# Every matmul operand in SBUF at one offset: split weights in tiles of 4096 bytes, SBUF pools in another order, a pad ahead of them

## The chip, the cores and the metric

The kernel runs on one core of a Trainium2 chip. The metric is the device time of one execution in microseconds (us), the median of several runs. The profile is one further execution, taken by the hardware profiler.

## The reference

A batch of one, 512 tokens by 1024 features, goes through two layers of a hybrid block and then one block of a second kind. All arrays are float32.

```python
# first block, twice (l = 0, 1)
mod = silu(c) @ w_ada[l] + b_ada[l]; shift, scale, gate = split(mod, 3)
h = rms_norm(x, norm_g[l]) * (1 + scale) + shift
gq, gk, gv, glr, gz, dq, dk, dv, dz = split_columns(h @ w_in[l])
gq, gk, gv = split(silu(causal_depthwise_conv([gq, gk, gv], conv_w[l])))
o_gla  = gla_branch(gq, gk, gv, glr, gz, ...)     # gated linear attention, chunks of 64
o_diff = diff_branch(dq, dk, dv, dz, ...)         # softmax maps p0 - lam * p1, 4 heads
x = x + gate * ([o_gla, o_diff] @ w_out[l])
# second block, once
x = x + 0.5 * swiglu(rmsnorm(x, ffn1_norm), ffn1_w_in, ffn1_w_out)      # D_FF = 2816
x = x + hybrid_mixer(rmsnorm(x, mix_norm), w_in, ..., w_out)
x = x + 0.5 * swiglu(rmsnorm(x, ffn2_norm), ffn2_w_in, ffn2_w_out)
return rmsnorm(x, final_norm)
```

Nearly all of the arithmetic lies in the products with weights: w_in and w_out of the two layers, the two feed-forwards, and the seven projections of the mixer.

## The kernel before

**Products in three passes.** A float32 product is made of three float32r matmuls (`mm3`, lines 163 to 167). Every operand is split in a high and a low part; the three are high by high (L165), one low by high (L166 or L167), and the other. The activations are split by `split` into slots, tiles of 512 float32 (2048 bytes) of the pool `sp`. The weights come in 1 MB transfers, one for each job, into tiles of the pool `wraw`, and `weights` (lines 131 to 145) splits them in pieces: ScalarE writes the high part (L141), VectorE the low part (L142), into two tiles of the pool `wsp`, tags `hi` and `lo`, four buffers each.

**Two forms of product.** In `fm1` (feature-major, tiles named `fm`) the stationary operand is a slice of 128 columns, 512 bytes, of a weight piece, and the moving operand a slot of activations of 512 columns. In `tm` (token-major, tiles named `tm`) it is the other way: a quarter of a slot is stationary, and 512 (or 264) columns of a weight piece move. A piece of a usual job is 8 slices of 128 columns in `fm1`, so 24 matmuls of 512 columns; in `tm` it is 2 slices by 4 token tiles by 3, also 24.

**Order.** `run` interleaves one stream of large products with light tasks (attention, linear attention, norms, modulation), by costs and due times in the code; the order of the instructions on each engine is then set by the tile scheduler. While job i runs, the pieces of job i + 1 are loaded and split. A new `hi` or `lo` tile waits until the matmuls on its buffer's earlier contents are done.

**Where the operands lie.** SBUF is given out in the order of the pools: `const`, `xp`, `wraw`, `wsp`, `sp`, `small`. An address here is the byte in each partition, as it stands in the built program. The slots of `sp` begin at 120736 and follow each other by 2048 bytes, so that each is 416 modulo 512. A `hi` or `lo` tile has 1056 columns, 4224 bytes, which is 8 x 512 + 128, so its four buffers begin at four different places modulo 512:

| buffer | before | modulo 512 | after the change | modulo 512 |
|---|---|---|---|---|
| hi | 86944, 91168, 95392, 99616 | 416, 32, 160, 288 | 45472, 49568, 53664, 57760 | 416, 416, 416, 416 |
| lo | 103840, 108064, 112288, 116512 | 416, 32, 160, 288 | 61856, 65952, 70048, 74144 | 416, 416, 416, 416 |
| slots | 120736 + 2048 n | 416 | 78240 + 2048 n | 416 |

The slices of a piece follow each other by 512 bytes (2048 in `tm`), so a whole piece keeps its place modulo 512. From the first feed-forward on the buffers are taken in turn: `hi` at 86944 (416), 99616 (288), 95392 (160), 91168 (32), and again. The `lo` part lies at 416 and 288 where `hi` does, at 32 where `hi` is at 160, and at 160 where `hi` is at 32.

**The odd width.** The 1056 columns are those of a piece of `wvg` (value projection and low-rank gate input, two jobs in each layer): a job has two pieces of 4 x 264 columns, `[(4, 264)] * 2`.

Of the kernel before, what the change touches and what calls it, by code (L numbers as in the profile page):

```python
# [16 lines left out]
P = 128  # L17
# [10 lines left out]
# columns of the packed vectors, each 128 values down the partitions  # L28
# [38 lines left out]
LG = 4.5  # L67


@with_exitstack  # L70
def block_kernel(ctx: ExitStack, tc: tile.TileContext, a, out):
# [3 lines left out]
    wraw = ctx.enter_context(tc.tile_pool(name="wraw", bufs=RAW))  # L75
    wsp = ctx.enter_context(tc.tile_pool(name="wsp", bufs=4))
    sp = ctx.enter_context(tc.tile_pool(name="sp", bufs=SLOTS))
    small = ctx.enter_context(tc.tile_pool(name="small", bufs=8))
    pp = ctx.enter_context(tc.tile_pool(name="pp", bufs=8, space=bass.MemoryType.PSUM))
    # the tensor engine takes its products in the order in which they are written here  # L80
# [45 lines left out]
    # 1 + the bias of the scale  # L126
# [4 lines left out]
    def weights(src, shapes, eng=V):  # L131
        """pieces [128, kts, n] of one transfer, each in its two parts; and the pieces themselves"""
        total = sum(k * n for k, n in shapes)
        raw = wraw.tile([P, 2112], F32, tag="raw", name=nm("raw"))
        nc.sync.dma_start(raw[:, 0:total], src)
        at, pieces = 0, []
        for k, n in shapes:
            src_p = raw[:, at:at + k * n]
            hi = wsp.tile([P, 1056], F32R, tag="hi", name=nm("hi"))[:, 0:k * n]
            lo = wsp.tile([P, 1056], F32R, tag="lo", name=nm("lo"))[:, 0:k * n]  # L140
            A.activation(hi, src_p, AF.Copy)  # L141
            eng.tensor_tensor(lo, src_p, f(hi), op=ALU.subtract)  # L142
            pieces.append(tuple(v.rearrange("p (k n) -> p k n", n=n) for v in (hi, lo, src_p)))
            at += k * n
        return pieces
# [4 lines left out]
    def split(src, s="sp", width=S, scale=None):  # L150
        """float32 tile -> its two parts; `scale`: a column that multiplies it"""
        hi = slot(s + "h", F32R)
        lo = slot(s + "l", F32R)
        h, l = hi[:, 0:width], lo[:, 0:width]
        if scale is None:
            A.activation(h, src, AF.Copy)
            V.tensor_tensor(l, src, f(h), op=ALU.subtract)
        else:
            A.activation(h, src, AF.Copy, scale=scale)
            V.scalar_tensor_tensor(l, src, scale, f(h), op0=ALU.mult, op1=ALU.subtract)  # L160
        return hi, lo

    def mm3(o, wh, wl, ah, al, start, stop):
        """o += (wh + wl).T @ (ah + al), without wl.T @ al: 2 ** -24 of a product, its rounding in float32"""
        T.matmul(o, wh, ah, start=start, stop=False)  # L165
        T.matmul(o, wh, al, start=False, stop=False)  # L166
        T.matmul(o, wl, ah, start=False, stop=stop)  # L167

    # ---- the order of the tensor engine's work: one stream of large products, and light tasks
    # between them. Both are generators; they yield the time that their products take, the light  # L170
    # ones also the time (or the event) before they go on ----
# [39 lines left out]
    st = {}  # L211

    def rsqrt(o, src, n, scale):
        """o = (src * scale + EPS) ** -0.5, src in SBUF or PSUM"""
        m = tiny([P, 8], "rin", bufs=8)
        V.tensor_scalar(m[:, 0:n], src, scale, EPS, op0=ALU.mult, op1=ALU.add)  # L216
        G.tensor_tensor(o, m[:, 0:n], mhalf[:, 0:n], op=ALU.pow)  # L217
# [9 lines left out]
    def norm(d0, d1):  # L227
        """a light task: column form [tok, 4] and row form [128, tok] of the inverse root"""
        yield 0, d0
        acc = st["acc"]  # L230
        ps = psum("nps")
        for t in range(NT):
            T.matmul(ps[:, t:t + 1], acc[:, t * P:(t + 1) * P], ones[:, 0:1], start=True, stop=True)
        rs = tiny([P, NT], "rs", bufs=2)
        rsqrt(rs, ps[:, 0:NT], NT, 1.0 / D)
        st["rs"] = rs
        rh, rl = tiny([P, NT], "rh", F32R, bufs=2), tiny([P, NT], "rl", F32R, bufs=2)
        V.tensor_copy(rh, rs)
        V.tensor_tensor(rl, rs, f(rh), op=ALU.subtract)
        yield 0.9, d1  # L240
        pb = psum("nbc")
        for t in range(NT):
            for i, r in enumerate((rh, rl)):
                T.matmul(pb[:, t * P:(t + 1) * P], r[:, t:t + 1].to_broadcast([P, P]), identr, start=i == 0, stop=i == 1)
        st["pb"] = pb
        bc = slot("rsb")
        A.activation(bc, pb, AF.Copy)
        st["bc"] = bc
        yield 1.7, 0
# [25 lines left out]
    def residual(o, k, scale, nxt):  # L275
        """x += scale o; the sum of squares and what the next stage reads follow"""
        V.scalar_tensor_tensor(xs[k], o, scale, xs[k], op0=ALU.mult, op1=ALU.add)
        after(k, nxt)
# [12 lines left out]
    mods = [(const.tile([P, 24], F32, name=f"mod{l}"), const.tile([P, 8], F32, name=f"gs{l}")) for l in range(L)]  # L291

    def ada_load(l, j, parts=1):
        """the weights of two columns a partition, of features 128 j on and 128 (j + 1) on"""
        w = wraw.tile([P, 2112], F32, tag="raw", name=nm("ada"))[:, 0:2 * D].rearrange("p (i r) -> p i r", r=D)
        for i in range(0, 2, 2 // parts):
            n = 2 // parts
            nc.sync.dma_start(w[:, i:i + n], a["ada"][l, j // 2][:, i:i + n])
        return w
# [6 lines left out]
    def mod_of(l, j, w):  # L306
        """of features 128 (j % 8) on: the shift, 8 on the scale, 16 on the gate"""
        mod, gs = mods[l]
        t, i = dot(w), j - 8
        if 0 <= i < 8:  # L310
            V.scalar_tensor_tensor(
                gs[:, i:i + 1], t, bg1[:, 8 * l + i:8 * l + i + 1], col("norm_g", 8 * l + i), op0=ALU.add, op1=ALU.mult)
        else:
            V.tensor_tensor(mod[:, j:j + 1], t, col("b_ada", 24 * l + j), op=ALU.add)
        st["mod", l, j] = True

    def modulation(which, pause):
        """a light task"""
# [8 lines left out]
    def lambdas():  # L327
        """a light task"""
        lamv = const.tile([64, 8], F32, name="lamv")
        nc.sync.dma_start(lamv, a["lamv"])  # L330
        for l in range(L):
# [7 lines left out]
            # -lam  # L339
# [6 lines left out]
    def head_norm(o, z, zi, gcol, y, yi, scales=None):  # L346
        """`scales`: columns that multiply the head's values"""
# [26 lines left out]
    def layer_jobs(l):  # L374
# [6 lines left out]
        def vectors():  # L381
            # small scaled vectors
# [4 lines left out]
            # taps [tile, tap]; what the silu's halves and the query's scale need goes into them  # L387
# [7 lines left out]
        def feat(k, eng):  # L395
            """x times the inverse root and the scale; and the shift"""
# [5 lines left out]
        # q, k of the softmax branch: normed over each 64  # L402
# [32 lines left out]
        # -- the first product(s) --  # L435
        if l == 0:
            # x times gain goes in as the scales come; the shift's part follows
# [15 lines left out]
            def q_part(k0, k1):  # L453
                def body(_):
# [4 lines left out]
                    for k in range(k0, k1):  # L459
# [7 lines left out]
                        if k % 2 == 0:  # L467
                            w["wh"] = tuple(wsp.tile([P, 1056], F32R, tag=v, name=nm(v)) for v in ("hi", "lo"))
# [107 lines left out]
        else:  # L576
            # x times gain goes in before the norm is known; the norm and the shift's product follow
# [36 lines left out]
        # -- v of the softmax branch and the gates' low-rank input --  # L614
# [30 lines left out]
        jobs += [(a["wvg"][l, b], [(4, 264)] * 2, vjob(b)) for b in range(2)]  # L645

        # -- softmax attention --
# [6 lines left out]
        def attention():  # L654
            qk, r0 = {}, {}

            def scores(hd, i):
                n = (i + 1) * P
                es, rr = [], []
                # the two maps lie in different halves of the array and run side by side  # L660
# [7 lines left out]
                for m in range(2):  # L668
# [10 lines left out]
                    else:  # L679
                        # the second's weight against the first's  # L680
# [45 lines left out]
        # -- gated linear attention --  # L726
        def gla():
# [48 lines left out]
            for c in range(4):  # L776
# [12 lines left out]
                # states of two heads (64 + 64 partitions) after each chunk  # L789
# [34 lines left out]
        # -- the rest of the large products --  # L824
# [8 lines left out]
        def z_job(dst, j0):  # L833
            # 2 silu(z)
# [17 lines left out]
        # -- output: the heads that are ready first go first --  # L852
# [3 lines left out]
        def wo_job(c):  # L856
            def body(ps):
                if c < 2:
                    # four tiles at once, with the heads as they come
# [31 lines left out]
    def ffn_jobs(i, nxt):  # L891
# [31 lines left out]
        # the last two tiles of the last stage, and what follows, take one half of the tokens at a time  # L923
# [34 lines left out]
        def last_norm(hs, sqs):  # L958
            """tokens down the partitions"""
# [34 lines left out]
    def mixer_jobs():  # L994
# [76 lines left out]
        # tanh(z / 2) + 1, twice the sigmoid, times the projection of one branch  # L1071
# [76 lines left out]
def _pack(i):  # L1148
# [4 lines left out]
    def chunk(w):  # L1153
        """[K, n] -> [128, (K / 128) n]: what a partition reads lies together"""
# [3 lines left out]
    def tiles(w):  # L1158
        """the same for each 128 columns in turn"""
        return np.concatenate([chunk(w[:, j:j + P]) for j in range(0, w.shape[1], P)], axis=1)  # L1160

    def cv(v):
        """a vector, 128 values down the partitions"""
# [75 lines left out]
```

## Time and profile before

| | |
|---|---|
| time, median of 3 runs | 1765.99 us (1765.78 to 1766.84) |
| the profiled execution, span of its instructions | 1762.7 us |
| TensorE (PE) busy | 1730.3 us, 98% |
| weight loads (PEld) | 1409.5 us, 80% |
| VectorE (DVE), ScalarE (ACT), GpSimd (POOL) | 54%, 38%, 5% |
| bytes from HBM | 178.00 MB, 102 GB/s over the span |

The profile gives each instruction's start and duration. Matmuls are pipelined: one that is listed with 0.39 us is followed by the next some 0.23 us later. So what a stream of matmuls costs is read from the distance of their starts and not from their durations. A weight load stands under PEld, beside the matmul that runs at the time. The profiled execution's span is 3.3 us below the median of the runs, which is what lies around it.

### The profile page before, as it was taken

The page shows a single profiled execution, that of the slowest core. Times are in us where ns is not written, and L with a number is a line of the kernel's source. Part 1 is how long each engine was busy: PE and PEld are TensorE (multiplying, and loading weights), DVE is VectorE, ACT ScalarE, POOL GpSimd, SP SyncE. Part 2 cuts the span into 40 slices and gives each one's busy share as a digit, 9 for nine tenths or more (in the row PEclk, how much of TensorE's full clock was granted, in tenths as well). Part 3 has the DMA queues.
Part 4 walks back from the last instruction along what each step waited for, and adds up shares of the span by engine and source line. Part 5 has one row for each costly group of instructions (what it writes and reads, how often), then busy time and mean ns, then how long its engine had stood idle before and what let it go on. Part 6 is the DMA issues. An engine that isn't in the chain of part 4 may idle for free.

```text
span 1762.7 us, 20264 instructions
## 1 busy us (share of the span) xinstructions
PE 1730.3 (98%) x8218; PEld 1409.5 (80%) x8218; DVE 951.7 (54%) x1488; ACT 665.8 (38%) x1135; POOL 88.0 (5%) x71
## 2 busy tenths in 40 slices
PE   6999999999999999999999999999999999999998
PEld 5787788787788888888888888888888888888887
DVE  8888867867755443344453543454444544334433
ACT  4555564556564322222233422222223322222233
POOL 3110010510010000000000000000000000000000
PEclk9998999999999999999999999999999999999999
DMA  8533432421112212322233222222222222332111
GB/s 308 198 131 120 168 120 98 171 87 53 55 66 96 96 66 80 129 96 73 80 124 130 84 96 96 96 96 96 94 93 97 77 86 69 117 121 88 66 49 49
DMA packets 29278, 181.41 MB, mean 103 GB/s; under 512 B 3296, under 2 KB 3456, under 8 KB 11136
## 3 DMA queue, kind: packets, MB, share of 16 engines
q1 hardware_dynamic: 29184, 180.11, 28.5%
q8 instruction: 64, 1.05, 0.2%
q14 instruction: 30, 0.25, 0.0%
HBM read 178.00 MB, written 2.10 MB: 102 GB/s over the span
## 4 chain that ended last, share of the span: by engine, by line
PE 94%; DVE 3%; ACT 2%; DMA 1%; issue 0%; POOL 0%; SPq 0%; POOLq 0%; DVEq 0%; ACTq 0%
PE fm L165 26%; PE fm L167 26%; PE fm L166 26%; PE tm L165 3%; PE tm L167 3%; PE tm L166 3%; PE sc L665 2%; PE o L701 1%; DVE ada L303 1%; DVE lo L142 0%; PE go L818 0%; PE at L692 0%; PE ot L368 0%; PE sg L1048 0%; DMA x<-in_xT 0%
## 5 line engine op out<-in xcount | busy, mean ns | idle before, releaser
L141 ACT ACTIVATE hi<-raw 128x1024 fp32r<-128x1024 f32 (+3 forms) x300 | 300.9, 1005 | 832.2 <-PE fm L166 695.3
L142 DVE TENSOR_TENSOR lo<-raw,hi 128x1024 fp32r<-128x1024 f32 (+3 forms) x300 | 346.4, 1156 | 155.3 <-ACT hi L141 154.6
L167 PE MATMUL fm<-xgh,lo 128*128 128x512 f32 x1088 | 428.7, 394 | 0.0
L165 PE MATMUL fm<-xgh,hi 128*128 128x512 f32 x1088 | 428.1, 393 | 0.0
L166 PE MATMUL fm<-xgl,hi 128*128 128x512 f32 x1088 | 427.5, 393 | 0.0
L166 PEld LDWEIGHTS fm<-xgl,hi 128*128 128x128 f32 x1088 | 204.6, 188 | 47.1
L165 PEld LDWEIGHTS fm<-xgh,hi 128*128 128x128 f32 x1088 | 205.0, 188 | 46.2
L167 PEld LDWEIGHTS fm<-xgh,lo 128*128 128x128 f32 x1088 | 204.4, 188 | 46.4
L165 PE MATMUL fm<-fhh,hi 128*128 128x512 f32 (+1 forms) x374 | 142.0, 380 | 0.0
L167 PE MATMUL fm<-fhh,lo 128*128 128x512 f32 (+1 forms) x374 | 141.9, 381 | 0.0
L166 PE MATMUL fm<-fhl,hi 128*128 128x512 f32 (+1 forms) x374 | 141.8, 381 | 0.0
L908 DVE TENSOR_TENSOR fu<-fm,rsb 128x512 f32<-128x512 f32 x44 | 30.4, 691 | 149.5 <-PE fm L167 149.5
L165 PE MATMUL fm<-hh,hi 128*128 128x512 f32 x256 | 107.3, 422 | 0.0
L167 PE MATMUL fm<-hh,lo 128*128 128x512 f32 x256 | 102.9, 402 | 0.0
L166 PE MATMUL fm<-hl,hi 128*128 128x512 f32 x256 | 102.8, 402 | 0.0
L165 PEld LDWEIGHTS fm<-fhh,hi 128*128 128x128 f32 x374 | 70.7, 189 | 14.2
L166 PEld LDWEIGHTS fm<-fhl,hi 128*128 128x128 f32 x374 | 70.4, 188 | 14.3
L905 DVE TENSOR_TENSOR fg<-fm,rsb 128x512 f32<-128x512 f32 x44 | 30.4, 691 | 94.6 <-PE fm L167 94.6
L167 PEld LDWEIGHTS fm<-fhh,lo 128*128 128x128 f32 x374 | 70.4, 188 | 13.9
L217 POOL TENSOR_TENSOR rs<-rin,mhalf 128x4 f32<-128x4 f32 (+1 forms) x7 | 8.5, 1219 | 1249.7 <-DVE rin L216 1249.7
L165 PE MATMUL tm<-hi,hh 128*128 128x264 f32 (+1 forms) x192 | 63.2, 334 | 4.4 <-ACT hh L512 4.4
L303 DVE SCALAR_TENSOR_TENSOR ada<-ada,cact 128x1024 f32<-128x1024 f32 x48 | 61.2, 1310 | 6.1 <-DMA ada<-in_ada 6.1
(252 smaller groups left out, 2512.9 us busy)
## 6 DMA issues: line engine op xcount, KB each, us to landing
raw<-in_ffi SPq DMA_DIRECT2D x44, 1024.0 KB, 4.7
ada<-in_ada SPq DMA_DIRECT2D x23, 1024.0 KB, 4.8
raw<-in_ffo SPq DMA_DIRECT2D x32, 704.0 KB, 4.1
raw<-in_wfm SPq DMA_DIRECT2D x16, 1024.0 KB, 4.8
raw<-in_mgp SPq DMA_DIRECT2D x16, 1024.0 KB, 4.8
raw<-in_wo SPq DMA_DIRECT2D x8, 1024.0 KB, 4.8
raw<-in_mcx SPq DMA_DIRECT2D x8, 1024.0 KB, 4.8
raw<-in_wtm SPq DMA_DIRECT2D x6, 1024.0 KB, 4.8
```

The costliest lines, as they stand in the source:

```text
L141: A.activation(hi, src_p, AF.Copy)
L142: eng.tensor_tensor(lo, src_p, f(hi), op=ALU.subtract)
L165: T.matmul(o, wh, ah, start=start, stop=False)
L166: T.matmul(o, wh, al, start=False, stop=False)
L167: T.matmul(o, wl, ah, start=False, stop=stop)
L217: G.tensor_tensor(o, m[:, 0:n], mhalf[:, 0:n], op=ALU.pow)
L303: V.scalar_tensor_tensor(w, w, 1.0, cact, op0=ALU.mult, op1=ALU.mult, accum_out=t)
L665: T.matmul(pss[m][:, 0:n], qk[hd][0][p][r, i * P:(i + 1) * P], qk[hd][1][q_][r, 0:n], start=p + q_ == 0, stop=False)
L701: T.matmul(on[hd][:, i * P:(i + 1) * P], et[:, j * P:(j + 1) * P], vt[j][:, hd * P:(hd + 1) * P], start=j == 0, stop=j == i)
L905: V.tensor_tensor(g, os[0], st["bc"], op=ALU.mult)
L908: V.tensor_tensor(u, os[1], st["bc"], op=ALU.mult)
```

## The change

The tiles `hi` and `lo` have 1024 columns, 4096 bytes, in place of 1056. So that a piece of `wvg` fits, its jobs are cut in three pieces of 3, 3 and 2 x 264 columns. The pool `wraw` is made behind `sp` in place of ahead of `wsp`, and a tile of 192 columns that nothing uses stands at the end of the early constants. The loop in `q_part` that splits the first product's weights takes the new tile width too. Comments and docstrings are taken out, which moves the lines by up to 3 (L165 to L167 are L168 to L170 afterwards).

```diff
+PAD = 192
@@ block_kernel
-    wraw = ctx.enter_context(tc.tile_pool(name="wraw", bufs=RAW))
     wsp = ctx.enter_context(tc.tile_pool(name="wsp", bufs=4))
     sp = ctx.enter_context(tc.tile_pool(name="sp", bufs=SLOTS))
+    wraw = ctx.enter_context(tc.tile_pool(name="wraw", bufs=RAW))
     small = ctx.enter_context(tc.tile_pool(name="small", bufs=8))
...
     cact = const.tile([P, D], F32, name="cact")
+    const.tile([P, PAD], F32, name="pad")
@@ weights
-            hi = wsp.tile([P, 1056], F32R, tag="hi", name=nm("hi"))[:, 0:k * n]
-            lo = wsp.tile([P, 1056], F32R, tag="lo", name=nm("lo"))[:, 0:k * n]
+            hi = wsp.tile([P, 1024], F32R, tag="hi", name=nm("hi"))[:, 0:k * n]
+            lo = wsp.tile([P, 1024], F32R, tag="lo", name=nm("lo"))[:, 0:k * n]
@@ q_part
-                            w["wh"] = tuple(wsp.tile([P, 1056], F32R, tag=v, name=nm(v)) for v in ("hi", "lo"))
+                            w["wh"] = tuple(wsp.tile([P, 1024], F32R, tag=v, name=nm(v)) for v in ("hi", "lo"))
@@ layer_jobs
-        jobs += [(a["wvg"][l, b], [(4, 264)] * 2, vjob(b)) for b in range(2)]
+        jobs += [(a["wvg"][l, b], [(3, 264), (3, 264), (2, 264)], vjob(b)) for b in range(2)]
```

The third piece adds one ScalarE and one VectorE instruction to each of the four `wvg` jobs, and the scheduler's order changes around them in the two layers. From the first feed-forward on every engine has the same order as before. The first place is ScalarE's queue in layer 0, where the two `wvg` jobs' pieces (`hi`, from a `raw` tile) are split, among the norms (`qn`, `qu`), the evacuations of the values (`vt`) and the pieces of the job behind them. Before:

```order
L141 ACTIVATE hi_529<-raw_523 128x1056
L141 ACTIVATE hi_756<-raw_754 128x1056
L558 ACTIVATE gku_706<-fm_406 128x512
L141 ACTIVATE hi_760<-raw_754 128x1056
...
L404 ACTIVATE qn_745<-qu_716 128x512
L141 ACTIVATE hi_894<-raw_892 128x1024
...
L337 ACTIVATE le_847<-lam_845 128x2
L623 ACTIVATE vt_764<-tm_768 128x264
```

The same place with the change:

```order
L144 ACTIVATE hi_530<-raw_524 128x792
L144 ACTIVATE hi_534<-raw_524 128x528
L561 ACTIVATE gku_711<-fm_407 128x512
L144 ACTIVATE hi_761<-raw_759 128x792
...
L407 ACTIVATE qn_750<-qu_721 128x512
L144 ACTIVATE hi_765<-raw_759 128x792
...
L340 ACTIVATE le_856<-lam_854 128x2
L144 ACTIVATE hi_769<-raw_759 128x528
L626 ACTIVATE vt_773<-tm_777 128x264
L626 ACTIVATE vt_774<-tm_778 128x264
L626 ACTIVATE vt_775<-tm_779 128x264
L626 ACTIVATE vt_776<-tm_780 128x264
```

The second `wvg` job's second and third pieces (`hi_765`, `hi_769`) have moved behind the norms, and the next job's first piece (before: `hi_894`, ahead of `vt`) comes only behind the four evacuations.

The second place is TensorE's queue in layer 0, some 130 us into the program, between a head's scores (`sc`), the attention's values (`o`) and a large product (`fm`). Before:

```order
L667 MATMUL sc_1257<-negr,rowm 128x64
L701 MATMUL o_1254<-vt_764,at_1214 128x128
L701 MATMUL o_1254<-vt_765,at_1214 128x128
L165 MATMUL fm_1306<-hh_415,hi_1102 128x512
L166 MATMUL fm_1306<-hl_416,hi_1102 128x512
...
L165 MATMUL fm_1306<-hh_553,hi_1102 128x512
L692 MATMUL at_1313<-ident,e_1151 128x128 x3
L166 MATMUL fm_1306<-hl_554,hi_1102 128x512
```

The same place with the change:

```order
L670 MATMUL sc_1266<-negr,rowm 128x64
L168 MATMUL fm_1315<-hh_416,hi_1111 128x512
L169 MATMUL fm_1315<-hl_417,hi_1111 128x512
...
L169 MATMUL fm_1315<-hl_588,hi_1111 128x512
L170 MATMUL fm_1315<-hh_587,lo_1112 128x512
L704 MATMUL o_1263<-vt_773,at_1223 128x128
L695 MATMUL at_1322<-ident,e_1160 128x128 x3
L704 MATMUL o_1263<-vt_774,at_1223 128x128
```

The two matmuls on values and the three transposes (`at`) stand behind 18 matmuls of the large product now, where before the first two stood ahead of it. The number of matmuls on the engine is the same.

## Rows read from the trace of the kernel before

**Rows 1.** The page: the span, and busy time of TensorE and its weight loads.

```profile
span 1762.7 us, 20264 instructions
PE 1730.3 (98%) x8218; PEld 1409.5 (80%) x8218; DVE 951.7 (54%) x1488; ACT 665.8 (38%) x1135; POOL 88.0 (5%) x71
```

**Rows 2.** The page: the chain of work that ended last, by engine.

```profile
PE 94%; DVE 3%; ACT 2%; DMA 1%; issue 0%; POOL 0%; SPq 0%; POOLq 0%; DVEq 0%; ACTq 0%
```

**Rows 3.** Windows by stage: stretch, length, busy us, granted clock, DMA share, GB/s.

```profile
0.00:160.00 160.00, 137.38 (x667) 111.31 (x668) 133.67 (x257) 86.04 (x146) 30.84 (x29) 0.94 0.54 199
160.00:560.00 400.00, 396.76 (x2235) 319.36 (x2234) 291.45 (x568) 220.54 (x536) 49.74 (x33) 1.00 0.28 102
560.00:1700.00 1140.00, 1140.00 (x4988) 929.44 (x4987) 505.65 (x631) 338.87 (x421) 6.02 (x7) 1.00 0.26 93
```

**Rows 4.** Timeline of TensorE, first feed-forward: first matmul of six successive pieces.

```profile
596.24 0.39 PE L165 MATMUL fm<-xgh,hi 128*128 128x512 f32 x1
...
601.68 0.40 PE L165 MATMUL fm<-xgh,hi 128*128 128x512 f32 x1
...
607.27 0.39 PE L165 MATMUL fm<-xgh,hi 128*128 128x512 f32 x1
...
612.84 0.40 PE L165 MATMUL fm<-xgh,hi 128*128 128x512 f32 x1
...
618.45 0.39 PE L165 MATMUL fm<-xgh,hi 128*128 128x512 f32 x1
...
623.90 0.40 PE L165 MATMUL fm<-xgh,hi 128*128 128x512 f32 x1
```

**Rows 5.** Groups of TensorE's instructions by line and shape: count, busy us, mean ns.

```profile
L165 PE MATMUL fm<-xgh,hi 128*128 128x512 f32 x1088 | 428.1, 393 | 0.0
...
L165 PE MATMUL fm<-fhh,hi 128*128 128x512 f32 x330 | 129.5, 392 | 0.0
...
L165 PE MATMUL fm<-hh,hi 128*128 128x512 f32 x256 | 107.3, 422 | 0.0
...
L165 PE MATMUL tm<-hi,xgh 128*128 128x512 f32 x128 | 50.6, 412 | 11.9 <-ACT hi L470 11.9
...
L165 PE MATMUL fm<-yh,hi 128*128 128x512 f32 x128 | 50.2, 397 | 0.0
...
L165 PE MATMUL tm<-hi,hh 128*128 128x512 f32 x64 | 27.1, 423 | 4.4 <-ACT hh L512 4.4
...
L165 PE MATMUL fm<-ybh,hi 128*128 128x512 f32 x64 | 25.3, 395 | 0.0
```

**Rows 6.** Timeline of TensorE in the mixer: first matmul of five token-major pieces.

```profile
947.48 0.40 PE L165 MATMUL tm<-hi,xgh 128*128 128x512 f32 x1
...
953.08 0.39 PE L165 MATMUL tm<-hi,xgh 128*128 128x512 f32 x1
...
958.66 0.39 PE L165 MATMUL tm<-hi,xgh 128*128 128x512 f32 x1
...
964.18 0.40 PE L165 MATMUL tm<-hi,xgh 128*128 128x512 f32 x1
...
969.66 0.40 PE L165 MATMUL tm<-hi,xgh 128*128 128x512 f32 x1
```

**Rows 7.** Waits of TensorE: us in total, times, longest.

```profile
PE tm L167 <- DVE hl L157: 3.2, 2, 1.6
PE at L692 <- DVE e L685: 2.5, 1, 2.5
```

**Rows 8.** Windows of TensorE in layer 0: stretch, length, busy us, granted clock.

```profile
120.00:140.00 20.00, 20.00 (x88) 0.91 0.44 156
140.00:160.00 20.00, 16.44 (x60) 0.74 0.39 134
```

**Rows 9.** Groups by line and shape: VectorE's split of weights.

```profile
L142 DVE TENSOR_TENSOR lo<-raw,hi 128x1024 fp32r<-128x1024 f32 x228 | 279.6, 1228 | 88.9 <-ACT hi L141 88.2
...
L142 DVE TENSOR_TENSOR lo<-raw,hi 128x640 fp32r<-128x640 f32 x32 | 26.2, 817 | 0.0
```

## The prediction

> **What bounds the kernel now.** I read the page's busy times first: TensorE is busy for 1730.3 of 1762.7 us and has 8218 matmuls [rows 1]. A busy TensorE need not be at its best, so I went on. The chain of work that ended last is TensorE for 94% [rows 2]. The windows by stage say where nothing else holds it up: from 560 to 1700 us it is busy in all 1140 us at the full granted clock, with DVE and ACT busy in 506 and 339 of them. Ahead of that it is different: up to 160 us DVE is busy for 133.67 of 160 us and TensorE for 137.38, and from 160 to 560 us TensorE waits for 3.2 us in all [rows 3]. So two thirds of the time is a stream of matmuls whose spacing is the time, and the question is what sets the spacing.
>
> The timeline answers it. In the first feed-forward the starts of successive pieces, 24 matmuls of 512 columns each, stand at 596.24, 601.68, 607.27, 612.84, 618.45 and 623.90 us [rows 4]. The pieces last 5.44, 5.59, 5.57, 5.61 and again 5.45 us. Same line, same shapes, same activations, nothing waited for: only the weight buffers differ. By the addresses in the table above, the short piece is the one whose high and low part both lie at 416 modulo 512, where the moving slots lie too. The others lie at 288, 160 and 32. Per matmul that is 226.9 ns (5.445 / 24) against 232.9, 232.1 and 233.8 ns. The order of length returns with the rotation, and as a piece's slices follow each other by 512 bytes, the place modulo 512 is what a whole piece shares.
>
> The token-major products say the same with the roles exchanged: there the weights move and the slots at 416 are stationary. The starts 947.48, 953.08, 958.66, 964.18 and 969.66 us [rows 6] are pieces at 288, 160, 32 and 416, of 5.60, 5.58, 5.52 and 5.48 us. So neither the place of the moving operand alone nor that of the stationary one alone gives the short piece; it is short where the two agree.
>
> **The change, part by part.**
>
> *Weights at 416.* In all, a rotation of four pieces lasts 618.45 - 596.24 = 22.21 us for 96 matmuls. Four short ones would last 4 x 5.445 = 21.78 us: 0.43 us less. The number of feature-major matmuls of 512 columns comes from the groups [rows 5]: 1088 (xgh), 330 (fhh), 256 (hh), 128 (yh) and 64 (ybh, and two more groups of 64 of the mixer), 1994 for L165, and three passes of each, 5982. Of these 3 x (256 + 128) = 1152 are in the two layers. The other 4830 make 50.3 rotations, mostly in the stretch where TensorE never waits: 50.3 x 0.43 = 21.6 us.
>
> *The same in the layers.* 1152 matmuls are 12 rotations, at most 5.2 us. But in layer 0 DVE is late: TensorE waits 2.5 us for attention weights (`e`), and in layer 1 twice 1.6 us for activations (`hl`) [rows 7]. What TensorE gains ahead of such a wait, it waits longer. The ends are 0 (all swallowed) and 5.2 us (none); I take the middle, 2.6 us.
>
> *Token-major.* The rotation 947.48 to 969.66 us is 22.18 us against 4 x 5.48 = 21.92: 0.26 us in 96 matmuls. There are 3 x (128 + 64) = 576 of them [rows 5], 6 rotations, 1.6 us at most; the first product waits for its weights for 11.9 us anyway, so I take 1.0 us. The ends are 0 and 1.6.
>
> *The third piece of `wvg`.* Four more splits on ACT and on DVE. A DVE split takes 1228 ns for 1024 columns and 817 ns for 640 [rows 9]: 1.07 ns a column, so some 0.13 us of one is fixed. Four are 0.5 us, on an engine that sets the pace in layer 0; charged in full, 0.5 us. Behind it lies a wait: two jobs now ask for six of four buffers, so the second job's second piece waits until the first job's first is done, and ACT's queue behind it with it. In the order shown these splits stand behind norms, and ahead of the values' evacuations (`vt`), which wait for the end of the first job anyhow; the buffers wanted are free earlier than that. I charge nothing more. If that cover is gone, TensorE waits as it now waits in layer 0.
>
> *Order in the layers and the clock.* From 120 to 160 us the granted clock is 0.91 and 0.74 [rows 8]: part of the time at 1.2 in place of 2.4 GHz, in the stretch that holds the wait for `e`. Where the small products fall moves a little with the new order. At 0.74 of the clock some half of 20 us runs at the lower level; that costs about 5 us at most, which may be saved or paid once more. I take 0 and keep 5 us on either side for the range.
>
> *Pools and pad.* They move addresses and issue nothing; the transfers are the same, and at a share of 0.26 of the DMA engines [rows 3] no transfer is waited for in the long stretch.
>
> Sum: -21.6 - 2.6 - 1.0 + 0.5 = -24.7 us. The profiled span of 1762.7 would be 1738.0; with the 3.3 us around it 1741.3 us. I say 1741.
>
> **A rule against it.** The rows show weight loads busy for 80% of the span beside a busy TensorE [rows 1], and pieces that differ by 0.17 us with the place of their weights [rows 4]. The Trainium skill, "TensorE: Matmul & The Clock Gate", Part 2, step by step, says that TensorE has two independent read ports, one for the moving operand and one for the weight load, and that loading the next weights steals no read bandwidth from the running matmul. By this rule the place of one operand against the other changes nothing and the sum is 0, apart from the splits; by the rows it is -24.7. The traces here do not agree with the rule, so it gets a small chance.
>
> **Rivals.**
>
> 1. *No gain: the two reads don't disturb each other, and the short piece is a property of one pair of buffers, not of its place modulo 512.* For it speaks that in the long stretch the high part at 416 is always the same buffer, 86944. Against it speaks that there are two parts in two buffers (86944 and 103840), and that in the token-major pieces the same place is the shortest with exchanged roles. It gives 1766.0 + 0.5 = 1766.5 us.
> 2. *Half a gain: the place within a larger unit counts too.* The moving slots begin at 1952 modulo 2048 before and at 416 after, a place that no moving operand had in this trace. If new pieces lay in the middle between the short and the mean one, the sum is -12.4 + 0.5: some 1754 us.
> 3. *Slower: equal places collide.* If at the new place two reads met in the same unit at every matmul, all pieces would be as long as the longest shown, 5.61 us. The rotation would be 22.44 in place of 22.21 us, 0.23 us more; over 5982 / 96 = 62.3 rotations that is 14.3 us: 1766.0 + 14.3 + 0.5 = 1780.8 us. It decides as soon as the mean piece is longer than 5.553 us (22.21 / 4). Against it: the slices of the short piece meet the slots at every multiple of 512 bytes already, without a long one.
>
> **How the numbers follow.** The forecast has a chance of 0.85, the half gain 0.06, no gain 0.05, slower 0.04. Within the forecast the bounds are: all terms at their best, -(21.6 + 5.2 + 1.6) = -28.4, and a clock stretch of 5 us saved, 1733; all swallowed in the layers and the clock stretch paid twice, -21.6 + 0.5 + 5, 1750. The outermost of these need several ends together, so the range is 1735 to 1750, which leaves out the three rivals (0.15) and little of the forecast. A measurement of this kernel can tell some 0.2% (3.5 us) from no change. Faster by more: the forecast and the half gain, 0.91. Within it: no gain, 0.05. Slower: 0.04.
>
> **What would show it.** In the first feed-forward all pieces should be 5.44 to 5.45 us apart and a rotation 21.78 us; token-major pieces 5.48. The stretch from the first feed-forward to the end should be shorter by some 22 us, and that ahead of it by 0 to 5. If single pieces still differ with their buffer, rival 1 is right; if all are equal but longer than 5.45, rival 2 or 3. If the pieces are short and the time isn't, look at the waits for `hi`, `lo`, `hl` and `e` in the layers, at ACT's queue behind `hi_765`, and at the granted clock between 100 and 170 us.

## The result, and the profile after

The changed kernel takes 1743.52 us (median of 4, 1741.81 to 1746.51) against 1765.88 us before (1765.33 to 1766.84): a ratio of 0.9877, interval 0.9863 to 0.9891, or 22.4 us less. The forecast was 1741, range 1735 to 1750. The total came out as forecast; two of its terms did not, and in part they cancel: that the total lies within 3 us of the forecast is partly luck.

The changed kernel's page: span and busy times, and the chain that ended last by engine and by line. The profiled execution, 1746.51 us, is the slowest of the four.

```profile
span 1744.7 us, 20274 instructions
...
PE 1710.6 (98%) x8218; PEld 1411.2 (81%) x8218; DVE 951.9 (55%) x1492; ACT 666.7 (38%) x1139; POOL 85.7 (5%) x71
...
PE 92%; DVE 3%; DMA 2%; ACT 2%; issue 1%; POOL 0%; SPq 0%; POOLq 0%; DVEq 0%; ACTq 0%
PE fm L168 26%; PE fm L170 26%; PE fm L169 26%; PE tm L168 3%; PE tm L170 3%; PE tm L169 3%; PE sc L668 1%; DMA ada<-in_ada 1%; DVE ada L306 1%; PE o L704 1%; DVE lo L145 1%; PE go L821 0%; PE ot L371 0%; PE at L695 0%; PE sg L1051 0%
```

As many matmuls as in [rows 1], in 19.7 us less of busy TensorE. But its share of the chain has fallen from 94 to 92% [rows 2], and the chain now has a transfer of modulation weights (`ada`) in it and the instruction of VectorE (L306) that reads it. That is the first sign of a new wait. The windows by stage (stretch, length, busy us of PE, PEld, DVE, ACT and POOL, granted clock, DMA share, GB/s) say where to look:

```profile
0.00:160.00 160.00, 139.77 (x696) 113.78 (x697) 136.03 (x265) 88.53 (x151) 29.78 (x29) 0.94 0.56 202
160.00:560.00 400.00, 392.67 (x2183) 316.61 (x2183) 286.04 (x563) 216.96 (x532) 48.55 (x33) 0.98 0.28 98
560.00:1700.00 1140.00, 1140.00 (x5087) 945.87 (x5086) 515.39 (x645) 347.80 (x433) 5.99 (x7) 1.00 0.27 94
```

In the long stretch TensorE is busy throughout at the full clock, as before, and gets through 5087 matmuls where it had 4988 [rows 3]: 2% more. From 160 to 560 us it is worse than before: 392.67 us busy against 396.76, and a granted clock of 0.98 against 1.00.

The timeline of TensorE in the first feed-forward, the first matmuls of four successive pieces of 24, to be held against [rows 4]:

```profile
584.82 0.39 PE L168 MATMUL fm<-xgh,hi 128*128 128x512 f32 x1
...
590.26 0.39 PE L168 MATMUL fm<-xgh,hi 128*128 128x512 f32 x1
...
595.70 0.39 PE L168 MATMUL fm<-xgh,hi 128*128 128x512 f32 x1
...
601.14 0.39 PE L168 MATMUL fm<-xgh,hi 128*128 128x512 f32 x1
```

Every piece lasts 5.44 us, 226.7 ns a matmul, where before only one piece of four did. The token-major pieces of the mixer (against [rows 6], 5.48 to 5.60 us) do the same:

```profile
947.07 0.39 PE L168 MATMUL tm<-hi,xgh 128*128 128x512 f32 x1
...
952.51 0.39 PE L168 MATMUL tm<-hi,xgh 128*128 128x512 f32 x1
...
957.95 0.39 PE L168 MATMUL tm<-hi,xgh 128*128 128x512 f32 x1
```

TensorE's waits in the layers (engine, line, what for: us in total, times, longest):

```profile
PE tm L170 <- DVE hl L160: 2.7, 2, 1.8
PE at L695 <- DVE cv L432: 2.5, 1, 2.5
PE sc L668 <- DVE zt L844: 1.3, 1, 1.3
PE sc L668 <- DVE cv L432: 1.3, 1, 1.3
```

The wait for `hl` is nearly what it was [rows 7]. The one of 2.5 us is not the one for `e` of before, which stood at 147 us and has shrunk to 0.9 us: it is a new wait, at 204 us. Of the two of 1.3 us, the one for `zt`, at 169 us, is new too; the other, at 145 us, stands where `sc` waited 1.1 us for `mod` before. The new waits lie between 160 and 320 us. The windows of this stretch, before and with the change:

```profile
160.00:320.00 160.00, 160.00 (x902) 128.46 (x901) 127.16 (x261) 85.16 (x221) 15.89 (x13) 1.00 0.39 142
...
160.00:320.00 160.00, 155.38 (x850) 124.38 (x850) 119.57 (x254) 79.69 (x214) 11.74 (x10) 0.97 0.35 128
```

Where TensorE was never idle before, it is idle for 4.6 us now.

### The profile page after: what moved, and what is told of

It reads as the page before. It is cut to its first block, busy times and chain, and to the rows that moved or that the text cites. A ratio compares the mean times of both kernels' runs of the same rounds, so it can differ in the third digit from the quotient of the medians.

```text
span 1744.7 us, 20274 instructions
## 1 busy us (share of the span) xinstructions
PE 1710.6 (98%) x8218; PEld 1411.2 (81%) x8218; DVE 951.9 (55%) x1492; ACT 666.7 (38%) x1139; POOL 85.7 (5%) x71
## 4 chain that ended last, share of the span: by engine, by line
PE 92%; DVE 3%; DMA 2%; ACT 2%; issue 1%; POOL 0%; SPq 0%; POOLq 0%; DVEq 0%; ACTq 0%
PE fm L168 26%; PE fm L170 26%; PE fm L169 26%; PE tm L168 3%; PE tm L170 3%; PE tm L169 3%; PE sc L668 1%; DMA ada<-in_ada 1%; DVE ada L306 1%; PE o L704 1%; DVE lo L145 1%; PE go L821 0%; PE ot L371 0%; PE at L695 0%; PE sg L1051 0%
## 5 line engine op out<-in xcount | busy, mean ns | idle before, releaser
L168 PE MATMUL fm<-xgh,hi 128*128 128x512 f32 x1088 | 424.2, 390 | 0.0
L169 PE MATMUL fm<-xgl,hi 128*128 128x512 f32 x1088 | 423.0, 389 | 0.0
L170 PE MATMUL fm<-xgh,lo 128*128 128x512 f32 x1088 | 423.0, 389 | 0.0
L170 PEld LDWEIGHTS fm<-xgh,lo 128*128 128x128 f32 x1088 | 204.2, 188 | 42.6
L168 PEld LDWEIGHTS fm<-xgh,hi 128*128 128x128 f32 x1088 | 204.3, 188 | 42.1
L168 PE MATMUL fm<-fhh,hi 128*128 128x512 f32 (+1 forms) x374 | 140.9, 377 | 0.0
L170 PE MATMUL fm<-fhh,lo 128*128 128x512 f32 (+1 forms) x374 | 140.2, 377 | 0.0
L168 PE MATMUL fm<-hh,hi 128*128 128x512 f32 x256 | 108.0, 425 | 0.8 <-ACT e L677 0.8
L170 PE MATMUL fm<-hh,lo 128*128 128x512 f32 x256 | 103.5, 404 | 0.0
L168 PEld LDWEIGHTS fm<-fhh,hi 128*128 128x128 f32 x374 | 70.4, 188 | 12.9
L170 PEld LDWEIGHTS fm<-fhh,lo 128*128 128x128 f32 x374 | 70.4, 188 | 12.9
L168 PE MATMUL tm<-hi,hh 128*128 128x264 f32 (+1 forms) x192 | 64.0, 338 | 4.4 <-ACT hh L515 4.4
L306 DVE SCALAR_TENSOR_TENSOR ada<-ada,cact 128x1024 f32<-128x1024 f32 x48 | 61.3, 1309 | 11.9 <-DMA ada<-in_ada 11.8
```

The lines of the kernel that those rows point to most:

```text
L306: V.scalar_tensor_tensor(w, w, 1.0, cact, op0=ALU.mult, op1=ALU.mult, accum_out=t)
```

## The experiments

Three things were open. **Theory A:** matmuls are short where stationary and moving operand agree in their place. **Theory B:** they are short because of the place 416 as such. **Theory C:** the third piece of `wvg`, with the order of instructions that comes with it, costs more than the 0.5 us it was charged, so that the alignment gave more than the total shows. For the spacing, each experiment is read as the time between the starts of two matmuls of a high by a high part (L165 before; the line's number differs from kernel to kernel) 32 slices (96 matmuls) apart in the first feed-forward; before, a rotation of 96 took 22.21 us [rows 4].

**Both operands at 0.** The changed kernel with a longer pad: weights and slots all begin at 0 modulo 512.

```diff
-PAD = 192
+PAD = 216
```

> Weights and slots all begin at 0 modulo 512, in place of 416; order of instructions as in the changed kernel. Theory A (what counts is that the two operands agree modulo 512): pieces of the first feed-forward stay 5.44 us apart, time 1743 us, give or take 3. Theory B (the place 416 itself is good, or these buffers): pieces longer, 5.55 us or more, time 1760 us or more.

Measured: 1745.14 us (1743.73 to 1749.28) against 1764.90 on the same chip, ratio 0.9894 (0.9878 to 0.9911). 96 matmuls in 21.76 us, as at 416. Theory B falls: the place itself does not matter.

**Weights moved by 128 against the slots.** The changed kernel with the pad 128 bytes longer and a pool of 96 columns between weights and slots, so that the slots stay at 416 modulo 512 and all the weights stand at 32.

```diff
-PAD = 192
+PAD = 224
     wsp = ctx.enter_context(tc.tile_pool(name="wsp", bufs=4))
+    gap = ctx.enter_context(tc.tile_pool(name="gap", bufs=1))
+    gap.tile([P, 96], F32, name="gap")
     sp = ctx.enter_context(tc.tile_pool(name="sp", bufs=SLOTS))
```

> Slots stay at 416 modulo 512, all eight weight buffers begin at 32, 128 bytes further; order as in the changed kernel. Theory A: every piece is long, 5.55 to 5.62 us, a rotation 22.2 to 22.5 us, time about 1768 us (1743.5 and 62 rotations of 0.4 us). Theory B, by the addresses of single buffers: pieces may differ from buffer to buffer, or stay at 5.44 us since all weights lie alike.

Measured in one run: 1780.21 us. The timeline, two matmuls 32 slices apart:

```profile
589.76 0.39 PE L170 MATMUL fm<-xgh,hi 128*128 128x512 f32 x1
...
612.08 0.39 PE L170 MATMUL fm<-xgh,hi 128*128 128x512 f32 x1
```

22.32 us, 232.5 ns a matmul: now every piece is long. Against the changed kernel, whose slots lie at the same place modulo 512, only the place of the weights differs, and the time is 36.7 us longer (35.1 us against both at 0). Theory A stands. The expected 1768 us is missed by 12: a rotation costs 0.56 us more than the changed kernel's, not the 0.4 it was taken for, and there are 62 of them.

**Aligned, with two pieces of `wvg`.** The changed kernel with tiles of 1152 columns (4608 bytes, 9 x 512), wide enough for two pieces; two slots fewer make room. On every engine the instructions then stand in the order of the kernel before.

```diff
-SLOTS = 50
+SLOTS = 48
-            hi = wsp.tile([P, 1024], F32R, tag="hi", name=nm("hi"))[:, 0:k * n]
-            lo = wsp.tile([P, 1024], F32R, tag="lo", name=nm("lo"))[:, 0:k * n]
+            hi = wsp.tile([P, 1152], F32R, tag="hi", name=nm("hi"))[:, 0:k * n]
+            lo = wsp.tile([P, 1152], F32R, tag="lo", name=nm("lo"))[:, 0:k * n]
...
-        jobs += [(a["wvg"][l, b], [(3, 264), (3, 264), (2, 264)], vjob(b)) for b in range(2)]
+        jobs += [(a["wvg"][l, b], [(4, 264)] * 2, vjob(b)) for b in range(2)]
```

> All operands at 416 modulo 512 as in the changed kernel, but with weight tiles of 1152 columns (4608 bytes, 9 x 512), so that the wvg jobs keep their two pieces and every engine has the order of the kernel before; 48 slots in place of 50 make the room. Theory C (the new order in the layers costs what the change fell short of, by more waits and more time at the lower clock): 1739 to 1741 us, waits as before. Theory D (a faster TensorE meets the same late DVE in the layers, whatever the order): 1743 us.

Measured: 1737.46 us (1736.72 to 1738.35), ratio 0.9844 (0.9829 to 0.9858). That is 6.1 us below the change, outside the changed kernel's own spread, and the gain is 5.1 us larger when each is held against the kernel before that was run beside it (1764.90 here, 1765.88 there). It is also below the 1739 to 1741 us that theory C expected. Its windows of the layers:

```profile
0.00:160.00 160.00, 137.86 (x670) 112.02 (x671) 133.89 (x257) 86.66 (x147) 30.36 (x29) 0.93 0.55 200
160.00:560.00 400.00, 396.70 (x2249) 321.70 (x2249) 293.97 (x572) 222.06 (x539) 49.50 (x33) 1.00 0.28 102
```

TensorE is idle for 560 - 137.86 - 396.70 = 25.4 us of them; before it was 25.9 [rows 3].

**Three pieces in the kernel before.** Nothing of the alignment, only the third piece; the instructions stand in the order of the changed kernel.

```diff
-        jobs += [(a["wvg"][l, b], [(4, 264)] * 2, vjob(b)) for b in range(2)]
+        jobs += [(a["wvg"][l, b], [(3, 264), (3, 264), (2, 264)], vjob(b)) for b in range(2)]
```

> The kernel before with the wvg jobs in three pieces and nothing else: its order is that of the changed kernel, its weight buffers lie at four places as before. Theory C: slower than before by 2 to 4 us, 1768 to 1770. Theory D: 1766 us, no difference that can be told. Both: pieces of the first feed-forward as before, 5.45, 5.59, 5.57, 5.61 us.

Measured: 1770.95 us (1770.48 to 1772.40) against 1764.90, ratio 1.0035 (1.0022 to 1.0049): 6.0 us slower, where theory C expected 2 to 4 and theory D none. Theory C is right in its direction, and its size was too small. Windows, and waits of TensorE and of VectorE, of this kernel:

```profile
0.00:160.00 160.00, 135.35 (x673) 109.64 (x674) 133.93 (x260) 86.63 (x148) 30.17 (x29) 0.95 0.55 200
160.00:560.00 400.00, 392.35 (x2202) 314.95 (x2201) 287.42 (x565) 219.21 (x535) 48.72 (x33) 1.00 0.28 99
...
PE at L692 <- DVE e L685: 2.6, 1, 2.6
PE at L692 <- DVE cv L429: 2.6, 1, 2.6
PE fm L165 <- ACT e L674: 1.5, 2, 0.8
...
DVE ada L303 <- DMA ada<-in_ada: 12.6, 11, 2.4
```

TensorE is idle for 560 - 135.35 - 392.35 = 32.3 us, 6.4 more than before, and the span is 6.5 us longer. The greater part of the 6.4 us lies between 160 and 320 us:

```profile
160.00:320.00 160.00, 155.50 (x866) 123.77 (x865) 120.18 (x253) 80.99 (x216) 10.47 (x9) 0.99 0.36 126
```

That is 4.5 us of idle time where the kernel before has none. The same stretch tells the two orders apart in every run of this case: TensorE is busy for all 160.00 us of it in the three kernels with two pieces (before, the third and the last experiment), and for 155.4 to 156.9 us in the eight with three, whatever the place of the operands. Some of the rest is chance: at the start of the program, ahead of the third piece, the first product waits 14.3 us for its weights here, 11.9 in the kernel before and 13.8 in the third experiment, all in the same order.

VectorE waits for modulation weights 11 times, 12.6 us; in the kernel before it was 6.1 us in 6. What has changed is seen some 200 us into the program. In the kernel before, VectorE finishes the attention weights (`e`) and the taps of the convolution (`cv`), and only then multiplies the modulation weights (`ada`):

```profile
196.03 0.48 DVE L685 SCALAR_TENSOR_TENSOR e<-e,r,e 128x256 f32<-128x256 f32 x1
196.42 0.74 DVE L429 SCALAR_TENSOR_TENSOR cv<-fm,cw,cv 128x509 f32<-128x509 f32 x1
...
198.86 1.22 DVE L303 SCALAR_TENSOR_TENSOR ada<-ada,cact 128x1024 f32<-128x1024 f32 x1
```

With three pieces the product stands ahead of them. The timeline of VectorE and, behind the second dots, of TensorE:

```profile
197.69 1.23 DVE L303 SCALAR_TENSOR_TENSOR ada<-ada,cact 128x1024 f32<-128x1024 f32 x1 [1.18 <-DMA ada<-in_ada]
198.84 0.48 DVE L685 SCALAR_TENSOR_TENSOR e<-e,r,e 128x256 f32<-128x256 f32 x1
...
204.02 0.74 DVE L429 SCALAR_TENSOR_TENSOR cv<-fm,cw,cv 128x509 f32<-128x509 f32 x1
205.98 1.23 DVE L303 SCALAR_TENSOR_TENSOR ada<-ada,cact 128x1024 f32<-128x1024 f32 x1 [1.22 <-DMA ada<-in_ada]
...
204.91 0.41 PE L692 MATMUL at<-ident,e 128*128 128x128 f32 x2 [2.56 <-DVE cv L429]
206.10 0.60 PE L165 MATMUL fm<-hh,hi 128*128 128x512 f32 x1 [0.78 <-ACT e L674]
206.50 0.63 PE L166 MATMUL fm<-hl,hi 128*128 128x512 f32 x1
```

The modulation product stands at the head of VectorE's queue and its transfer has not landed. VectorE stands still for 1.2 us, then does this product and others; the last tap of the convolution comes at 204.02 us in place of 196.42, and TensorE waits 2.6 us for it. Not all of these 2.6 us are the transfer's: the wait for it is 1.2 us, and the rest is work that now stands ahead of the tap. After that TensorE's matmuls start some 0.42 us apart for a while, at the lower level of the clock (1.2 GHz; the granted clock of the 20 us from 200 on is 0.91, and it is 1.00 there in the kernel before). The transfers are not issued later than before: SP issues these two at 192.72 and 201.15 us here, at 193.91 and 201.26 in the kernel before. What has changed is the order of the instructions, on VectorE and, as the text ahead of the prediction shows, on TensorE itself. How much of the 4.5 us each has was not tried.

**Only the low parts moved by 128.** The changed kernel with the `lo` tiles in a pool of their own, at 32 modulo 512; `hi` tiles and slots stay at 416. Two theories of the mechanism are told apart: **A1**, the load of the next weights disturbs the matmul beside it, and **A2**, a matmul is longer on weights that were loaded from another place.

```diff
+    gap = ctx.enter_context(tc.tile_pool(name="gap", bufs=1))
+    gap.tile([P, 32], F32, name="gap")
+    wlp = ctx.enter_context(tc.tile_pool(name="wlp", bufs=4))
+    gap2 = ctx.enter_context(tc.tile_pool(name="gap2", bufs=1))
+    gap2.tile([P, 96], F32, name="gap2")
...
-            lo = wsp.tile([P, 1024], F32R, tag="lo", name=nm("lo"))[:, 0:k * n]
+            lo = wlp.tile([P, 1024], F32R, tag="lo", name=nm("lo"))[:, 0:k * n]
```

> High parts and slots at 416 modulo 512, the low parts alone 128 bytes further (32); order as in the changed kernel. Theory A1 (a matmul is slowed by the weight load that runs beside it, so by the place of the next matmul's weights): in the feed-forward L168 (next load: high) 226.7 ns, L169 (next load: low) some 232 ns, L170 (its own weights are the low part, next load: high) 226.7 ns. Theory A2 (by the place of its own weights): L170 232 ns, the other two 226.7. Both: pieces some 5.48 to 5.50 us, time about 1753 us (a third of the distance from 1744 to 1780, some 12 us more, less what is chance in the layers).

Measured in one run: 1770.70 us (1765.23 for the kernel before beside it), 96 matmuls in 22.18 us. By line, as means of the time to the next start over all steady feature-major matmuls: L173 (own weights high, the next load high) 226.7 ns, L174 (own high, the next load low) 232.5, L175 (own low, the next load high) 234.2. Both misses: neither theory alone gives two long matmuls. L174 is long though only the load beside it is out of place; L175 is long though only its own weights are. One misplaced part of three costs 13.3 ns in a group of three, all three (second experiment) 17.4, and so the time missed the expected 1753 us too.

The token-major pieces of the same run say more. There the weights move, and every load is of a slot, which lies in place; only the moving low part is out of place. In the mixer the three matmuls of a group take 235 (L173, high part moving), 235 (L174, low part) and 230 ns (L175, high part), against 227, 227 and 226 in the changed kernel. All three are long and no load is misplaced: theory A1 can't be the whole cause. What one misplaced operand does reaches the matmuls beside it.

**Moved by 32, 64 and 256.** As the second experiment, with a pad and a gap of 200 and 120 columns, 208 and 112, 256 and 64.

```diff
-PAD = 192
+PAD = 256
+    gap = ctx.enter_context(tc.tile_pool(name="gap", bufs=1))
+    gap.tile([P, 64], F32, name="gap")
```

> Weights at 448, slots at 416 modulo 512, 32 bytes apart; order as in the changed kernel. If any disagreement counts: 231 ns or more a matmul, 1770 to 1780 us. If only a larger unit counts (64 bytes or more): 226.7 to 228 ns, about 1744 us.

> Weights at 480, slots at 416 modulo 512, 64 bytes apart; order as in the changed kernel. If any disagreement counts: 231 ns or more, 1770 to 1780 us. If a unit of 128 bytes counts: 226.7 to 228 ns, about 1744 us.

> Weights at 160, slots at 416 modulo 512, 256 bytes apart; order as in the changed kernel. By the kernel before, whose pieces with a part at 160 took 232.1 ns a matmul beside low parts at 32: 230 to 233 ns and 1765 to 1780 us. If the unit is 256 bytes: 226.7 ns and 1744 us.

Measured in one run each: 1782.39, 1782.86 and 1740.66 us, against the same 1765.23. The timeline with the weights moved by 32, then by 256:

```profile
590.27 0.40 PE L170 MATMUL fm<-xgh,hi 128*128 128x512 f32 x1
...
612.67 0.40 PE L170 MATMUL fm<-xgh,hi 128*128 128x512 f32 x1
```

```profile
590.54 0.39 PE L170 MATMUL fm<-xgh,hi 128*128 128x512 f32 x1
...
612.30 0.39 PE L170 MATMUL fm<-xgh,hi 128*128 128x512 f32 x1
```

| weights against slots | 96 matmuls, us | ns a matmul |
|---|---|---|
| 0 (both at 416, both at 0) | 21.76 | 226.7 |
| +32 | 22.40 | 233.3 |
| +64 | 22.40 | 233.3 |
| +128 | 22.32 | 232.5 |
| +256 | 21.76 | 226.7 |
| +128, low parts only | 22.18 | 231.0 |

At +256, where the expectation leaned to long pieces, they are short. By these offsets the unit is 256 bytes and not 512; 96, 160, 192 and 224 bytes were not tried. By a unit of 256, half of the tiles before were well placed (160 is 416 modulo 256), but only one pair, 416 with 416, had both parts so; `hi` at 160 went with `lo` at 32 and the other way round.

**The kernel before with tiles of 4352 bytes.** If 256 is the unit, a tile of 17 x 256 bytes is enough, with nothing else changed: two pieces, old pools, every instruction where it stood. The tiles begin at 160 or 416 modulo 512.

```diff
-            hi = wsp.tile([P, 1056], F32R, tag="hi", name=nm("hi"))[:, 0:k * n]
-            lo = wsp.tile([P, 1056], F32R, tag="lo", name=nm("lo"))[:, 0:k * n]
+            hi = wsp.tile([P, 1088], F32R, tag="hi", name=nm("hi"))[:, 0:k * n]
+            lo = wsp.tile([P, 1088], F32R, tag="lo", name=nm("lo"))[:, 0:k * n]
...
-                            w["wh"] = tuple(wsp.tile([P, 1056], F32R, tag=v, name=nm(v)) for v in ("hi", "lo"))
+                            w["wh"] = tuple(wsp.tile([P, 1088], F32R, tag=v, name=nm(v)) for v in ("hi", "lo"))
```

> The kernel before with its weight tiles made 1088 columns (4352 bytes) long in place of 1056 (4224 bytes), and nothing else: two pieces of wvg, the pools in their old order, every instruction where it stood. The high and low parts then begin at 160 or 416 modulo 512, the activations' slots at 416, so all agree modulo 256, and only half of the tiles agree with the slots modulo 512. If 256 bytes is the unit (as the weights moved by 256 showed): every steady piece of 512 columns at 226.7 ns a matmul, the stretch from matmul no. 3200 to no. 8100 at 1093 us, and the whole about 1737.5 us, as with the aligned kernel in two pieces. If 512 is the unit and the weights moved by 256 were fast for another reason: half of the rotations at 232 ns, the stretch about 1107 us, and the whole about 1751 us. If it were the new order of the pools that gave the gain: no change, 1765.

Measured: 1737.05 us (1735.81 to 1739.08) against 1765.22, ratio 0.9843 (0.9830 to 0.9857). The timeline, 32 slices apart, and the window of the long stretch:

```profile
590.16 0.39 PE L165 MATMUL fm<-xgh,hi 128*128 128x512 f32 x1
...
611.92 0.39 PE L165 MATMUL fm<-xgh,hi 128*128 128x512 f32 x1
...
560.00:1700.00 1140.00, 1140.00 (x5087) 946.27 (x5086) 512.72 (x641) 346.98 (x432) 5.99 (x7) 1.00 0.27 93
```

21.76 us again, and the same 5087 matmuls in the stretch as the changed kernel. 32 more columns in each tile, without the reordered pools, the pad and the third piece, give 28.2 us, 5.8 more than the change.

## Why the prediction was right, and which terms were not

The four kernels with and without alignment and third piece make a square of medians. The changed kernel's 1743.52 us is of another series, in which the kernel before took 1765.88; the other three were run together.

| | pieces at mixed places | all aligned | alignment |
|---|---|---|---|
| two pieces, old order | 1764.90 | 1737.46 | -27.4 |
| three pieces, new order | 1770.95 | 1743.52 | -27.4 |
| third piece and order | +6.0 | +6.1 | |

That the sums agree to 0.1 us is chance. With both operands at 0, the same order in the same series as the other three took 1745.14 us: by it the alignment gives 25.8 us and the third piece costs 7.7. What the table shows is that the alignment gives some 26 to 28 us with either order, and the third piece costs some 5 to 8 us at either place. By the prediction's steps:

- *Weights at 416, -21.6 us.* Right. From matmul no. 3200, some 66 us into the feed-forwards, to no. 8100, near the end, the traces show 1114.9 us before and 1093.2 us after. From the first matmul of the first feed-forward to the end of the program it is 1201.7 us before and 1178.8 after, 22.9 us less, and the same 1178.8 in the two aligned kernels with two pieces. The mixer's token-major matmuls are in it, some 1.7 us.
- *The same in the layers, -2.6, from 0 to -5.2.* Nearly the full gain. With the instructions in the old order the first feed-forward begins at 561.0 us before, and at 556.8 (third experiment) and 555.7 (last experiment) with all operands aligned: 4.2 and 5.4 us earlier, some of it token-major. Half was taken off because the waits for `hl` and `e` were to swallow it; the idle time of the layers stayed at 25.4 against 25.9 us in the third experiment.
- *Token-major, -1.0, from 0 to -1.6.* Too small. The pieces are 5.44 us, so that even the shortest piece before, 5.48, had not the aligned length; why not is open. A rotation of four falls from 22.18 [rows 6] to 21.76 us, 0.42 and not 0.26; over 6 rotations that is 2.5 us, 1.7 of them in the mixer. The size of the whole term was not measured apart from the others.
- *The third piece, +0.5.* This is the term that was mis-sized: it measured 6.0 us in the kernel before. The splits were counted, and the waits for weight buffers on ACT's queue, but not what the new order does elsewhere: on VectorE modulation products, whose transfers have not landed, stand ahead of attention weights and convolution. The prediction looked for trouble in ACT's queue and between 100 and 170 us; the new waits lie at 169 and 204 us.
- *Order and clock, 0 (5 either way).* Part of the changed kernel's loss lies here. In its profiled execution TensorE's idle time in the layers is 27.6 us, only 2.1 more than with two pieces; the span is 9.1 us longer, and the other 7 us are the clock's, 0.94 and 0.98 in the two windows against 0.93 and 1.00. This is its slowest execution: the four go with the mean clock, 0.993, 0.992, 0.990 and 0.989 gave 1741.81, 1742.41, 1744.63 and 1746.51 us, and by 0.991 in the middle against 0.993 before the clock costs some 3 us. In the profiled execution of the kernel before with three pieces the mean clock was 0.993, as with two, and the loss was all idle time. So the same 6 us are made up differently in the two.

The mechanism, that a matmul is short where its two operands agree in their place, was right, and its unit too coarse, 256 and not 512 bytes, which changes nothing in this kernel's sum, since all its operands agree modulo 512. Had it been known, two pieces in tiles of 4352 bytes would have been the change to make. The half gain (rival 2) and no gain (rival 1) fall with the timeline. Rival 3, long pieces everywhere, forecast 1780.8 us; at +128 the time is 1780.21, but the places are unequal there: the number agrees by chance, and the cause it named, equal places, gives short pieces.

The traces do not agree with what was drawn from the rule. The changed kernel and the second experiment, of 1743.52 and 1780.21 us, differ in the place of the weights against the slots alone, and a matmul of 512 columns takes 226.7 ns in one and 232.5 in the other. The Trainium skill, "TensorE: Matmul & The Clock Gate", Part 2, step by step, has it that loading the next weights takes no read bandwidth from the running matmul; for these float32r operands, at 32, 64 or 128 bytes from each other, the runs show that the place of one against the other sets the spacing all the same. Whether reads collide, or something else hangs on the place, is not settled: feature-major matmuls are long, 234.2 ns, with their own low part out of place and the load beside them in place, and token-major ones, 235 ns, with every load in place.

Nor does the place modulo 256 explain everything. The piece before with its high part at 160 and its low part at 32 took 232.1 ns a matmul, the fifth experiment, the same places modulo 256, 231.0. By line the piece before has 230.9, 231.8 and 233.9 ns (high by high, low activations by high, high by low), the experiment 226.7, 232.5 and 234.2: the difference lies in the matmul of the two high parts, and why it is long before is open.

## What to carry to other kernels

When same-shaped matmuls with no waits have two or more spacings that return with the buffers' rotation, print the operands' addresses and make tile lengths a multiple of the unit that they show (here 256 bytes) before anything else is changed. Here 32 more columns in each tile, with every instruction where it stood, gave as much (1737.05 us) as reordered pools, pad and longer tiles without the third piece (1737.46), and 5.8 us more than the change. An edit that looks like four extra splits on each of two engines can change a scheduler's order everywhere: compare the orders, look in the new one for instructions that wait on a transfer with critical work queued behind them, and try the two halves of such a change apart.

## What had not been expected of the hardware

A feature-major matmul of 512 float32r columns starts every 226.7 ns when stationary and moving operand lie 0 or 256 bytes apart modulo 512, and every 232.5 to 233.3 ns when all the weights lie 32, 64 or 128 bytes off: 2.5 to 2.9%, on TensorE at a granted clock of 1.00. Moving the weights by 32 bytes costs as much as by 64. Token-major pieces follow at 0 and 256 (5.44 us), 32 (5.60) and 128 (5.58), but at 64 they take 5.50 us, less than half of the loss; why is open. Nothing is shown of matmuls of 264 moving columns: their slices follow each other by 1056 bytes, 4 x 256 + 32, so that the places differ within a piece in every kernel here.
